# Block sums made in DRAM by accumulating transfers, and a fourth pair by seven products

## The chip, the cores and the metric

The kernel runs on one core of one Trainium2 chip. A core has five engines that run side by side, each with its own in-order queue: TensorE (PE, matrix products into PSUM), VectorE (DVE), ScalarE (ACT), GpSimd (POOL) and SyncE (SP, which here only issues transfers). Sixteen DMA engines move data between DRAM and SBUF for all queues. The metric is the time of one execution on the device in microseconds (us), the median of the runs; less is better.

## The reference

One layer of an encoder block on 256 tokens of width 2048, float32. What bears on the change is the output projection; everything else is shortened.

```
hn = rmsnorm(h, mix_norm_pre)
z, xbc, dt_raw, u = split(hn @ w_in)
y_ssd  = ssd_mixer(z, xbc, dt_raw, ...)        # 256 x 1024
y_pool = pool_mixer(u, pool_w, pool_scale)     # 256 x 1024
mix = concat([y_ssd, y_pool]) @ w_out          # 256 x 2048 times 2048 x 2048
h = h + rmsnorm(mix, mix_norm_post)
h = h + rmsnorm(conv_glu(rmsnorm(h, ...), w_up, w_down), ...)
h = h + rmsnorm(sigmoid(rmsnorm(h, ...) @ w_gate) * (p @ w_ple), ...)
```

## The kernel before

**Products.** Every float32 weight page is split into a high and a low part (ScalarE copies the high part, VectorE subtracts to get the low part, lines 157 and 158), and a product of x and w is three matmuls: high by high, high by low, low by high. A weight page is 128 partitions by 2048 columns, 1 MB; it holds a pair of contraction blocks of 128 rows by 1024 output columns, cut into four blocks of 512 columns. Three raw buffers (`raw`), five buffers for split weights (tag `w`), thirteen 1 MB pages (tag `pg`) hold the data.

**Plain pairs and pairs by seven products.** A plain pair takes 2 blocks x 2 token halves x 2 column blocks x 3 matmuls = 24 matmuls of 128x512. A pair may instead be done by a scheme of the Strassen and Winograd kind with seven block products, 21 matmuls (`seven_products`, line 277). That needs sums of the four weight blocks (`add_blocks`: block 1 += block 0; block 0 += block 3; block 3 += block 1; block 2 += block 3, in this order) and four sums of the operand (`pair_sums`). Its splits are named after the pair: a (block 1, 512 columns) and b (blocks 2 and 3) come from the raw page, d and c (the sums) from a second page `t` where the sums were made earlier, or else from the raw page after `add_blocks` has run over it. One combining step (`combine`) follows the last fast pair of a half.

**The output projection** (`wo`) runs as two halves of 1024 output columns, eight pairs each. The lists of pairs are numbered by their first block k; the second half goes through the blocks 8, 10, 12, 0, 2, 14, 4, 6. By seven products go the pairs 0 and 2 of the first half and 12, 0, 2 of the second. For four of these five the sums are made early, in the stages of `xbc` (the three slabs 2, 0, 1) and `z`: `early_fetch` loads the weight page into a page `wob`, `early_add` adds on VectorE (line 275) and stores the page to DRAM (`wos`, line 265, a GpSimd transfer); the projection loads it again as `wo00t`, `wo02t`, `wo10t`, `wo12t`. Pair 12 makes its sums in the projection itself, on its raw page `wo112r`.

**What sets the order.** `aside()` runs the next list of `work` after each pair of a stage, so a job's place in `work` says in which part of a stage it is written. The Tile scheduler then orders each engine's queue by priority. SyncE's loads also keep the order of `issue_after(last["dma"])`: a load that waits for a buffer holds those behind it. GpSimd's queue carries the stores, and between them the small instructions of the norms, among them `yn0m`, `yn0r`, `yn1m`, `yn1r` (lines 410 to 417 and 817), the norm of y: y is scaled by them on VectorE, turned by TensorE (`y_turn`, tile `yt`, line 827) and becomes the operand of the pairs 0 to 6.

Of the kernel before, what the change touches and what calls it, by code (L numbers as in the profile page):

```python
# [11 lines left out]
F32 = mybir.dt.float32  # L12
F32R = mybir.dt.float32r
AF = mybir.ActivationFunctionType
ALU = mybir.AluOpType
ORDERED = (mybir.EngineType.Activation, mybir.EngineType.DVE, mybir.EngineType.SP)

P = 128
# [20 lines left out]
V_MIX, V_SCW, V_SCB, V_SN, V_PS, V_FN = 0, 16, 76, 88, 96, 104  # L39
# [14 lines left out]
def build(nc, a, out):  # L54
    x = a["x"][0]

    w_dtu, w_xbc, w_z, w_out, w_up = a["w_dtu"], a["w_xbc"], a["w_z"], a["w_out_"], a["w_up"]
# [3 lines left out]
    with tile.TileContext(nc) as tc, \  # L61
# [9 lines left out]
        def ins(r):  # L71
            return getattr(r, "ins", r)

        def page(name, dtype=F32):
            return gp.tile([P, 2048], dtype, tag="pg", bufs=13, name=name)

        def mid(name, dtype=F32):
            return gp.tile([P, 1024], dtype, tag="mid", bufs=3, name=name)
# [4 lines left out]
        def main(name):  # L83
            return [pm.tile([P, 512], F32, tag="main", name=f"{name}_{i}") for i in range(2)]
# [30 lines left out]
        last, sums_ = {}, {}  # L115

        def load(dst, src, ahead=False):

            with tc.issue_after(last["dma"]) if last and not ahead else nullcontext():
                return ins(nc.sync.dma_start(dst, src))  # L120
# [79 lines left out]
        work = []  # L200
# [31 lines left out]
        def block_sums(name, w, c0, k, held):  # L232


            pg = []

            def fetch():
                r = page(f"{name}b{c0}_{k}")
                pg.append(r)
                load(r, w[c0 // 1024, k // 2])  # L240

            def add():
                add_blocks(pg[0])
                if held:
                    sums_[name, c0, k] = pg[0], True

            def store():
                if not held:
                    t = dp.tile([P, 2048], F32, tag=f"{name}s{c0}_{k}", bufs=1, name=f"{name}s{c0}_{k}")
                    nc.gpsimd.dma_start(t, pg[0])  # L250
                    sums_[name, c0, k] = t, False

            return fetch, add, store

        early_raw = {}

        def early_fetch(c, k):
            early_raw[c, k] = page(f"wob{c}_{k}")
            load(early_raw[c, k], w_out[c, k // 2])

        def early_add(c, k):
            r = early_raw.pop((c, k))
            add_blocks(r)
            t = dp.tile([P, 2048], F32, tag=f"wos{c}_{k}", bufs=1, name=f"wos{c}_{k}")
            nc.gpsimd.dma_start(t, r)
            sums_["wo", c * 1024, k] = t, False

        APART = ("dn",)

        def add_blocks(r, t=None):  # L270

            v = r.rearrange("p (b c) -> p b c", b=4)
            s = v if t is None else t.rearrange("p (b c) -> p b c", b=4)
            for i, a, b in ((1, v, 0), (0, v, 3), (3, s, 1), (2, s, 3)):
                nc.vector.tensor_add(s[:, i], v[:, i], a[:, b])  # L275
# [95 lines left out]
        def feature_major(name, w, get, acc):  # L371

            for u in range(4):
                r = raw(f"{name}r{u}", w[u])
                for j in range(2):
                    wh, wl = split(f"{name}{u}_{j}", r[:, j * 1024:(j + 1) * 1024], 1024)
                    for kk in range(2):
                        k = 4 * u + 2 * j + kk
                        xh, xl = get(k)
                        for f in range(4):  # L380
                            s = slice(kk * 512 + f * P, kk * 512 + (f + 1) * P)
                            for q, (ww, xx) in enumerate(((wh, xh), (wh, xl), (wl, xh))):
                                mm(acc[f // 2][:, f % 2 * L:(f % 2 + 1) * L], ww[:, s], xx,
                                   k == 0 and q == 0 and f % 2 == 0, k == NK - 1 and q == 2)
                aside()
# [19 lines left out]
        def rms(name, parts, scale, n=1):  # L405

            base = EPS
            for i, q in enumerate(parts):
                m = tiny(f"{name}m{i}", n)
                nc.gpsimd.tensor_scalar(m, q, scale, base, op0=ALU.mult, op1=ALU.add)  # L410
                base = m
            r = tiny(f"{name}r", n)
            nc.gpsimd.tensor_tensor(r, m, mhalf[:, :n], op=ALU.pow)
            return r
# [36 lines left out]
        def times_rows(name, acc, rb):  # L451
            o = mid(name)
            for i in range(2):
                nc.vector.tensor_tensor(o[:, i * 512:(i + 1) * 512].rearrange("p (f t) -> p f t", f=2),
                                        acc[i].rearrange("p (f t) -> p f t", f=2),
                                        rb.unsqueeze(1).to_broadcast([P, 2, L]), op=ALU.mult)
            return o

        def conv(name, acc, taps, wcol, wstep, bcol):

            cv = mid(name)
            half = taps // 2
            for f in range(4):
                o, i = cv[:, f * L:(f + 1) * L], acc[:, f * L:(f + 1) * L]
                nc.scalar.activation(o, i, AF.Identity, bias=vec(bcol + f), scale=vec(wcol + half * wstep + f))
                for j in range(taps):
                    d = j - half
                    if d == 0:
                        continue
                    lo, hi = max(0, -d), L - max(0, d)  # L470
                    nc.vector.scalar_tensor_tensor(o[:, lo:hi], i[:, lo + d:hi + d], vec(wcol + j * wstep + f),
                                                   o[:, lo:hi], op0=ALU.mult, op1=ALU.add)
            return cv
# [15 lines left out]
        for u in range(0, NK, 2):  # L489
            r = [wp.tile([P, 2048], F32, tag="raw", bufs=3, name=f"dtur{u}") if u else r0, page(f"dtur{u + 1}")]  # L490
            for j in range(2):
                k = u + j
# [17 lines left out]
            for j in range(2):  # L510
                k = u + j
# [129 lines left out]
        cat = Panel.__new__(Panel)  # L641
# [54 lines left out]
        def xbc(slab):  # L696
            acc = main(f"xbc{slab}")
            feature_major(f"xb{slab}", w_xbc[slab], hn, acc)
            sc = times_rows(f"xr{slab}", acc, rxb)
            cv = conv(f"cv{slab}", sc, 5, V_SCW + 4 * slab, 12, V_SCB + 4 * slab)  # L700
            th = mid(f"th{slab}")
            nc.scalar.activation(th, cv, AF.Tanh, scale=0.5)

            nc.vector.scalar_tensor_tensor(cv, th, 1.0, cv, op0=ALU.add, op1=ALU.mult)
            return cv
# [42 lines left out]
        def job(f, *args):  # L748
            return lambda: f(*args)
# [5 lines left out]
            [job(pool_mix, 2), job(pool_mix, 3), job(decays), job(seg_sums)],  # L755
            [],
        ])
        work[0].append(job(early_fetch, 0, 0))
        work[2].append(job(early_add, 0, 0))
        work[1].append(job(early_fetch, 0, 2))  # L760
        work[3].append(job(early_add, 0, 2))
        work[3].append(job(early_fetch, 1, 0))
        bc = xbc(2)
        work.extend([
            [job(seg, 0), job(seg, 1), job(pool_map, 0), job(pool_map, 1)],
# [1 line left out]
            [job(seg, 4), job(weigh, 0, 0), job(pool_map, 2)],  # L767
            [job(seg, 5), job(pool_map, 3)],
        ])
        work[0].append(job(early_add, 1, 0))  # L770
        xa = xbc(0)
        work.extend([
            [job(seg, 6)],
# [1 line left out]
            [job(xs_turn, xa, 0)],  # L775
            [],
        ])
        xb = xbc(1)
        y = page("y")

# [8 lines left out]
            [job(mix, 0, 1), job(mix, 1, 0)],  # L789
            [job(mix, 1, 1)],  # L790
        ])
        work[4].append(job(early_fetch, 1, 2))
        work[6].append(job(early_add, 1, 2))
        zacc = [main(f"z{t}") for t in range(2)]
        token_major("z", w_z, 0, list(range(NK)), hn, zacc)
        assert not work
# [5 lines left out]
        for t in range(2):  # L802
# [13 lines left out]
            r = rms(f"yn{t}", [ss], rz[t][:, 1:2], n=2)  # L816
# [16 lines left out]
        def gload(name, src):  # L833
            g = cp.tile([P, D], F32, tag="gain", name=name)
            load(g, src.partition_broadcast(P))
            return g
# [91 lines left out]
        for t in range(2):  # L928
            load(h[t], x[t * P:(t + 1) * P, :])
        hf = sublayer("wo", w_out, (list(range(8, 16)) + list(range(8)), [8,9,10,11,12,13,0,1,2,3,14,15,4,5,6,7]), cat, gload("gmix", a["mix_norm_post"][0]), h,  # L930
                      V_FN, Pairs, ((4,5),(2,3,4)), Sums("cs", cat))


        pl = [ple(0)]
# [39 lines left out]
        for i, w_ in enumerate(which[2:] + which[:2]):  # L974
            fetch, add, store = block_sums(*w_, i >= len(which) - 2)
            n = 45 * i // 10 + 4
# [110 lines left out]
        with in_order():  # L1087
            for _ in range(5):
                next_part()
            for n in range(NPIECES):  # L1090
                s, v, i = blocks[n // 4]
# [135 lines left out]
        for half in range(2):  # L1227
# [16 lines left out]
            for t in range(2):  # L1244
                for n, (o, c0) in enumerate(columns(acc[t])):
                    c1 = c0 + o.shape[-1]
                    c = slice(half * 1024 + c0, half * 1024 + c1)

                    th = mid(f"gth{half}{t}{n}")
                    v = th[:, :c1 - c0]  # L1250
# [103 lines left out]
```

## Time and profile before

| what | us |
|---|---|
| median of 3 runs (1105.19 to 1105.71) | 1105.4 |
| the profiled execution | 1104.97 |
| its span | 1103.2 |
| TensorE busy | 1096.7 |
| VectorE busy | 977.2 |
| ScalarE busy | 729.1 |
| GpSimd busy | 84.9 |

The span is what the profiler saw between the first and the last instruction; the time of the profiled execution is 1.8 us longer. The stages that the change touches lie between 50 and 284 us: xbc to about 141, z to 196, the first half of the projection to 241, the second half to 284. In a row of the profile, "out<-in" names the tiles that an instruction writes and reads, xN counts, and what stands in brackets is the idle time before it with what ended that time.

### The profile page before, as it was taken

How to read it: one execution, taken by the hardware profiler on the slowest of the kernel's cores; microseconds unless marked ns; L12 is line 12 of the kernel's file. 1: busy time of each engine (PE TensorE's matmuls, PEld its weight loads, DVE VectorE, ACT ScalarE, POOL GpSimd, SP SyncE). 2: the span in 40 equal slices, each digit the busy share in tenths (PEclk: the TensorE clock that was granted, in tenths of full speed). 3: DMA queues.
4: the chain of work that ended last, by engine and by line, in shares of the span. 5: the costliest groups of instructions: out<-in, count | busy, mean ns of one | idle time of the engine just before them, and what ended most of it. 6: DMA issues, size and time to landing. Idle time of an engine off the chain costs nothing.

```text
span 1103.2 us, 16052 instructions
## 1 busy us (share of the span) xinstructions
PE 1096.7 (99%) x5961; PEld 948.8 (86%) x5961; DVE 977.2 (89%) x1373; ACT 729.1 (66%) x1068; POOL 84.9 (8%) x145
## 2 busy tenths in 40 slices
PE   9999999999999999999999999999999999999998
PEld 9999988888888888888888888888888888888886
DVE  6589998898868998889889988898999999999997
ACT  6858763566776565655656646657688878786773
POOL 0200000100100000000000000000000000051001
PEclk9999999999999999999999999999999999999999
DMA  9895259556489999989999998999999989996872
GB/s 363 359 339 195 101 183 367 209 195 244 158 367 388 408 397 364 403 344 367 383 366 383 364 391 345 404 362 420 367 410 375 378 335 389 419 379 224 317 276 77
DMA packets 57247, 361.71 MB, mean 328 GB/s; under 512 B 6352, under 2 KB 7504, under 8 KB 21200
## 3 DMA queue, kind: packets, MB, share of 16 engines
q1 hardware_dynamic: 45648, 298.71, 69.0%
q0 software_dynamic: 11088, 61.35, 14.5%
q8 instruction: 47, 0.77, 0.3%
q10 hardware_dynamic: 432, 0.62, 0.2%
q14 instruction: 32, 0.26, 0.1%
HBM read 306.65 MB, written 54.00 MB: 327 GB/s over the span
## 4 chain that ended last, share of the span: by engine, by line
PE 97%; ACT 1%; DVE 1%; issue 0%; POOL 0%; POOLq 0%; DVEq 0%
PE ga L90 22%; PE va L90 22%; PE dna L90 11%; PE woa L90 7%; PE xbc L90 5%; PE gt L90 5%; PE dns L90 4%; PE dtu L90 4%; PE z L90 4%; PE dn0s L90 2%; PE dn1s L90 2%; PE ple L90 1%; PE gts L90 1%; PE wos L90 1%; PE yd L90 1%; PE pw L90 1%
## 5 line engine op out<-in xcount | busy, mean ns | idle before, releaser
L90 PE MATMUL ga<-wox,ug_0w 128*128 128x512 f32 x704 | 130.8, 337 | 0.0
L90 PE MATMUL ga<-wox,ug_1w 128*128 128x512 f32 x704 | 130.2, 337 | 0.0
L90 PE MATMUL va<-wox,uv_0w 128*128 128x512 f32 x704 | 129.2, 337 | 0.0
L90 PE MATMUL va<-wox,uv_1w 128*128 128x512 f32 x704 | 129.2, 337 | 0.0
L90 PEld LDWEIGHTS ga<-wox,ug_0w 128*128 128x128 f32 x704 | 107.7, 188 | 14.6 <-ACT pl L919 0.2
L90 PEld LDWEIGHTS ga<-wox,ug_1w 128*128 128x128 f32 x704 | 107.5, 188 | 14.5 <-DVE wox L195 0.2
L90 PEld LDWEIGHTS va<-wox,uv_1w 128*128 128x128 f32 x704 | 107.5, 188 | 14.5
L90 PEld LDWEIGHTS va<-wox,uv_0w 128*128 128x128 f32 x704 | 107.5, 188 | 14.5
L275 DVE TENSOR_TENSOR dnb<-dnb 128x512 f32<-128x512 f32 x128 | 88.3, 690 | 3.0
L250 POOL DMA_DIRECT2D dns<-dnb x30 | 16.1, 536 | 319.4 <-DVE dnb L275 279.1
L90 PE MATMUL xbc<-hnh,xb_0w 128*128 128x256 f32 x192 | 37.9, 284 | 0.3 <-ACT u L571 0.3
L90 PE MATMUL xbc<-hnh,xb_1w 128*128 128x256 f32 x192 | 37.1, 283 | 0.0
L846 ACT CAST he<-he 128x512 fp32r<-128x512 f32 x13 | 8.1, 621 | 42.6 <-DVE he L845 42.6
L988 ACT CAST hs<-hid 128x384 fp32r<-128x384 f32 (+1 forms) x44 | 23.4, 537 | 13.7 <-PE dna L90 13.5
L90 PEld LDWEIGHTS xbc<-hnh,xb_0w 128*128 128x128 f32 x192 | 30.8, 189 | 0.9 <-ACT u L571 0.4
L90 PEld LDWEIGHTS xbc<-hnh,xb_1w 128*128 128x128 f32 x192 | 30.7, 189 | 0.1
L1068 ACT ACTIVATE fc<-gr,vt 128x256 f32<-128x256 f32 x44 | 26.1, 593 | 6.9 <-DVE gr L1061 6.9
L90 PE MATMUL dna<-dn_0w,hs 128*128 128x512 f32 x108 | 28.6, 394 | 0.0
L90 PE MATMUL dna<-dn_1w,hs 128*128 128x512 f32 x108 | 28.3, 392 | 0.0
L1139 POOL DMA_DIRECT2D hd<-hsum x24 | 12.9, 539 | 193.1 <-PE dn0s L90 70.4
L989 DVE TENSOR_TENSOR hs<-hid,hs 128x384 fp32r<-128x384 f32 (+1 forms) x44 | 25.4, 581 | 2.6 <-ACT hs L988 2.6
L90 PE MATMUL xbc<-hnl,xb_1w 128*128 128x256 f32 x96 | 27.3, 284 | 0.0
(1781 smaller groups left out, 2871.4 us busy)
## 6 DMA issues: line engine op xcount, KB each, us to landing
dnb<-w_down SPq DMA_DIRECT2D x32, 1024.0 KB, 10.0
dns<-dnb POOLq DMA_DIRECT2D x30, 1024.0 KB, 6.5
hd<-hsum POOLq DMA_DIRECT2D x24, 512.0 KB, 8.2
zr<-w_z SPq DMA_DIRECT2D x8, 1024.0 KB, 5.0
dtur<-w_dtu SPq DMA_DIRECT2D x14, 528.0 KB, 8.5
hsum<-he POOLq DMA_DIRECT2D x13, 512.0 KB, 7.7
wo0r<-w_out_ SPq DMA_DIRECT2D x6, 1024.0 KB, 6.2
gtb<-w_gate SPq DMA_DIRECT2D x6, 1024.0 KB, 9.6
```

Of the source, the lines that this page charges most:

```text
L90: last["pe"] = ins(nc.tensor.matmul(o, lhsT, rhs, start=start, stop=stop, skip_group_check=True))
L250: nc.gpsimd.dma_start(t, pg[0])
L275: nc.vector.tensor_add(s[:, i], v[:, i], a[:, b])
L846: nc.scalar.copy(o[:, :512], s[:, :512])
L988: nc.scalar.copy(t[:, :c1], hid_part(k)[:, :c1])
L989: nc.vector.tensor_sub(t[:, 512:512 + c1], hid_part(k)[:, :c1], t[:, :c1].bitcast(F32))
L1068: nc.scalar.activation(c[:, f], v[:, f], AF.Identity, bias=vec(V_FCB + 4 * s + 2 * i + f), scale=vec(w + NF))
L1139: nc.gpsimd.dma_start(o.bitcast(F32), kept[k])
```

## The change

`early_fetch` and `early_add` go. In their place `sums_in_dram(c, k)` gives three jobs, placed in consecutive lists of `work`: a copy of the weight page from DRAM to DRAM (SyncE's queue), two accumulating transfers on GpSimd's queue that add block 3 to the copy's blocks 0 and 2 and block 0 to its blocks 1 and 3 (512 KB each), and two more that add block 1 of the copy to its block 2 and block 1 of the weights to its block 3 (256 KB each). VectorE and the pages `wob` are not used for it. It is done for six pairs: those four, pair 12 of the second half, and pair 10 of the second half, which is now done by seven products too.

```diff
-        def early_fetch(c, k):
-            early_raw[c, k] = page(f"wob{c}_{k}")
-            load(early_raw[c, k], w_out[c, k // 2])
-
-        def early_add(c, k):
-            r = early_raw.pop((c, k))
-            add_blocks(r)
+        def sums_in_dram(c, k):
             t = dp.tile([P, 2048], F32, tag=f"wos{c}_{k}", bufs=1, name=f"wos{c}_{k}")
-            nc.gpsimd.dma_start(t, r)
-            sums_["wo", c * 1024, k] = t, False
+            src = w_out[c, k // 2]
+            o, v = (u.rearrange("p (b c) -> p b c", b=4) for u in (t, src))
+
+            def add(dst, from_):
+                nc.gpsimd.dma_start(dst, from_, accum_op=ALU.add)
+
+            def copy():
+                load(t, src)
+
+            def pairs_():
+                add(o[:, 0::2], v[:, 3:4].to_broadcast([P, 2, 512]))
+                add(o[:, 1::2], v[:, 0:1].to_broadcast([P, 2, 512]))
+
+            def rest():
+                add(o[:, 2], o[:, 1])
+                add(o[:, 3], v[:, 1])
+                sums_["wo", c * 1024, k] = t, False
+
+            return copy, pairs_, rest
...
-        work[0].append(job(early_fetch, 0, 0))
-        work[2].append(job(early_add, 0, 0))
-        work[1].append(job(early_fetch, 0, 2))
-        work[3].append(job(early_add, 0, 2))
-        work[3].append(job(early_fetch, 1, 0))
+        for n, j in enumerate(sums_in_dram(0, 0)):
+            work[1 + n].append(j)
...
-        work[0].append(job(early_add, 1, 0))
+        for n, j in enumerate(sums_in_dram(0, 2)):
+            work[1 + n].append(j)
...
+        for n, j in enumerate(sums_in_dram(1, 0)):
+            work[1 + n].append(j)
...
-        work[4].append(job(early_fetch, 1, 2))
-        work[6].append(job(early_add, 1, 2))
+        for n, j in enumerate(sums_in_dram(1, 2)):
+            work[1 + n].append(j)
+        for n, j in enumerate(sums_in_dram(1, 10)):
+            work[5 + n].append(j)
+        for n, j in enumerate(sums_in_dram(1, 12)):
+            work[3 + n].append(j)
...
-                      V_FN, Pairs, ((4,5),(2,3,4)), Sums("cs", cat))
+                      V_FN, Pairs, ((4,5),(1,2,3,4)), Sums("cs", cat))
```

Two places in the queues. SyncE's loads for the second half of the projection, before (a name wo1NNr is the raw page of pair NN, wo1NNt its sums; wo1r are raw pages of plain pairs):

```order
L120 DMA wo1r_2468<-w_out_ 128x2048
L120 DMA wo1r_2500<-w_out_ 128x2048
L120 DMA wo112r<-w_out_ 128x2048
L120 DMA wo10r<-w_out_ 128x1536
L120 DMA wo12r<-w_out_ 128x1536
L120 DMA wo10t<-wos_0_1073 128x2048
L120 DMA wo12t<-wos_2_2005 128x2048
L120 DMA wo1r_2656<-w_out_ 128x2048
```

and in the changed kernel:

```order
L120 DMA wo1r_2472<-w_out_ 128x2048
L120 DMA wo110r<-w_out_ 128x1536
L120 DMA wo112r<-w_out_ 128x1536
L120 DMA wo10r<-w_out_ 128x1536
L120 DMA wo110t<-wos_10_1667 128x2048
L120 DMA wo112t<-wos_12_1668 128x2048
L120 DMA wo10t<-wos_0_1362 128x2048
L120 DMA wo12r<-w_out_ 128x1536
L120 DMA wo12t<-wos_2_1666 128x2048
```

The second pair of the half, 10, now has a page of sums, and its load stands behind three raw pages, the last of which takes the buffer of the half's first pair.

GpSimd's queue ahead of the norm of y, at the end of the z stage, before:

```order
L608 TENSOR_TENSOR dec<-dec,dt 128x16 x2
L265 DMA wos_2_926<-wob_2_763 128x2048
L265 DMA wos_0_1073<-wob_0_928 128x2048
L265 DMA wos_2_2005<-wob_2_1890 128x2048
L410 TENSOR_SCALAR yn0m_2069<-ss_2060,rz_2055 128x2
L413 TENSOR_TENSOR yn0r<-yn0m_2069,mhalf 128x2
```

and in the changed kernel:

```order
L262 DMA wos_2_1666<-w_out_ 256x1x512 x2
L262 DMA wos_2_1666<-wos_2_1666 128x512
L262 DMA wos_2_1666<-w_out_ 128x512
L262 DMA wos_12_1668<-w_out_ 256x1x512 x2
L262 DMA wos_12_1668<-wos_12_1668 128x512
L262 DMA wos_12_1668<-w_out_ 128x512
L262 DMA wos_10_1667<-w_out_ 256x1x512 x2
L262 DMA wos_10_1667<-wos_10_1667 128x512
L262 DMA wos_10_1667<-w_out_ 128x512
L420 TENSOR_SCALAR yn0m_2073<-ss_2064,rz_2059 128x2
L423 TENSOR_TENSOR yn0r<-yn0m_2073,mhalf 128x2
```

Twelve accumulating transfers of the three last blocks now stand ahead of `yn0m` in the z stage, each block's second two behind a wait for its first two, and its first two behind a wait for its copy; before, one store stood there.

More of the change, by code (lines that the diff above doesn't have):

```diff
@@ L253, in block_sums @@
             return fetch, add, store
-        early_raw = {}
-        def early_fetch(c, k):
-            early_raw[c, k] = page(f"wob{c}_{k}")
-            load(early_raw[c, k], w_out[c, k // 2])
-        def early_add(c, k):
-            r = early_raw.pop((c, k))
-            add_blocks(r)
-            t = dp.tile([P, 2048], F32, tag=f"wos{c}_{k}", bufs=1, name=f"wos{c}_{k}")
-            nc.gpsimd.dma_start(t, r)
-            sums_["wo", c * 1024, k] = t, False
+        def sums_in_dram(c, k):
+            t = dp.tile([P, 2048], F32, tag=f"wos{c}_{k}", bufs=1, name=f"wos{c}_{k}")
+            src = w_out[c, k // 2]
[12 more added lines that the diff above has]
+            return copy, pairs_, rest
         APART = ("dn",)
```

## The prediction

> **What bounds the kernel now.** I read the page first, then the chain of waits, then the table of windows, then the rows of single queues around the change.
>
> ```profile
> span 1103.2 us, 16052 instructions
> PE 1096.7 (99%) x5961; PEld 948.8 (86%) x5961; DVE 977.2 (89%) x1373; ACT 729.1 (66%) x1068; POOL 84.9 (8%) x145
> PE 97%; ACT 1%; DVE 1%; issue 0%; POOL 0%; POOLq 0%; DVEq 0%
> ```
>
> The chain that ended last is 97% TensorE. That is an average, so the stages that the change touches come from the windows (us; busy time and instructions of PE, PEld, DVE, ACT, POOL; granted clock; DMA share; GB/s):
>
> ```profile
> 50.00:64.00 14.00, 13.75 (x112) 13.55 (x111) 13.74 (x27) 9.39 (x13) 0.53 (x1) 1.00 0.68 261
> 64.00:79.00 15.00, 15.00 (x126) 14.53 (x125) 12.30 (x23) 6.49 (x10) 1.50 (x3) 1.00 0.96 358
> 79.00:90.00 11.00, 10.82 (x88) 10.46 (x87) 9.13 (x19) 10.96 (x17) 1.12 (x2) 1.00 0.73 282
> 90.00:120.00 30.00, 29.98 (x232) 28.89 (x231) 28.96 (x55) 23.39 (x46) 0.00 (x0) 1.00 0.39 135
> 120.00:141.00 21.00, 21.00 (x172) 20.55 (x171) 20.73 (x36) 13.47 (x25) 0.00 (x0) 1.00 0.40 142
> 141.00:163.00 22.00, 22.00 (x99) 17.97 (x98) 21.62 (x44) 15.79 (x30) 0.00 (x0) 1.00 0.45 168
> 163.00:175.00 12.00, 12.00 (x56) 9.72 (x55) 11.96 (x12) 4.98 (x6) 0.00 (x0) 1.00 0.94 371
> 175.00:186.00 11.00, 11.00 (x63) 8.98 (x61) 8.26 (x11) 3.14 (x3) 0.53 (x1) 1.00 0.87 333
> 186.00:197.00 11.00, 11.00 (x63) 9.14 (x62) 7.36 (x12) 4.97 (x9) 1.93 (x5) 1.00 0.58 223
> 241.00:284.00 43.00, 43.00 (x187) 34.76 (x186) 36.96 (x46) 25.32 (x33) 1.81 (x6) 1.00 0.68 255
> ```
>
> TensorE is full in every one of them: from 50 to 197 us it lacks 0.25 + 0.18 + 0.02 = 0.45 us in all, and in the second half of the output projection (241 to 284) nothing. VectorE is nearly as full in places (21.62 of 22). So time comes back only where TensorE has fewer products, and it is lost only where something makes TensorE wait that does not now.
>
> **Term 1, three products fewer.** The chain in the second half, start and length in us:
>
> ```profile
> 240.78 11.55 PE woa L90 x50
> 252.34 0.69 PE wos L90 x3
> 257.22 0.70 PE wos L90 x3
> ```
>
> A plain product takes 11.55 / 50 = 0.231 us, so a plain pair, 24 products, 5.54. The second and third row are the first products of pair 12 and of pair 0: a pair by seven products, 21 of them, lies 4.88 apart. Pair 10 goes from the one to the other: **-0.66 us**.
>
> **Term 2, VectorE's adds.** The change takes away both of these groups:
>
> ```profile
> L275 DVE TENSOR_TENSOR wob<-wob 128x512 f32<-128x512 f32 x16 | 11.0, 686 | 0.2
> L275 DVE TENSOR_TENSOR wo112r<-wo112r 128x512 f32<-128x512 f32 x4 | 2.7, 686 | 0.1
> ```
>
> The sixteen lie in the stages above, where TensorE is full anyway; all that they could give back is the 0.45 us, and I take 0. In the second half 2.7 us go, and pair 10 brings two more splits (0.7 + 3 x 1.22 against 2 x 1.22 us, by the split rows below) and its own operand sums (0.69 + 4 x 0.29 + 0.68, as pair 12 has them): about 1.9 + 2.5 - 2.7 = 1.7 us more for a VectorE with 6 us spare. Hidden, unless it comes late at the first fast pair, which is term 3.
>
> **Term 3, the first fast pair is one pair earlier and its sums are a load.** SyncE's issues, TensorE's gate and what the splits cost (start, length in us):
>
> ```profile
> 239.69 0.33 SPq L120 DMA_DIRECT2D wo10r<-w_out_  x1
> 243.50 0.42 SPq L120 DMA_DIRECT2D wo10t<-wos  x1
> wo10t<-wos SPq DMA_DIRECT2D x1, 1024.0 KB, 6.7
> wo02t<-wos SPq DMA_DIRECT2D x1, 1024.0 KB, 10.2
> 250.19 1.05 ACT L157 CAST wo112dw<-wo112r 128x1024 fp32r<-128x1024 f32 x1 [2.69 <-DVE wo112r L275]
> 251.27 1.22 DVE L158 TENSOR_TENSOR wo112dw<-wo112r,wo112dw 128x1024 fp32r<-128x1024 f32 x1 [1.17 <-ACT wo112dw L157]
> 253.54 0.68 DVE L158 TENSOR_TENSOR wo10aw<-wo10r,wo10aw 128x512 fp32r<-128x512 f32 x1
> ```
>
> In the new order wo110t is issued right behind wo10r, which waits for a raw buffer until 239.69. Issued at 240.1, and landing after 6.7 us as wo10t did behind a raw page, it is there at 246.8. TensorE reaches pair 10 at 252.34 - 5.54 = 246.8, and its first nine products (a11, a12, s4) need wo110r alone: the sums' first high part is wanted at 246.8 + 9 x 0.232 = 248.9, its low part four products later, at 249.8. ScalarE has the high part at 246.8 + 1.05 = 247.9, VectorE the low part at 249.1. That is 0.7 to 1.0 us of room. Behind it VectorE goes on with 112's splits, and by the same durations ends its third (112d) at about 253.1, where TensorE wants it at 253.5. So nothing to 1 us is lost; between these ends I take **+0.2 us**. The far end is a landing like wo02t's 10.2 us: 3.5 us later, 2.5 to 2.8 of them seen.
>
> **Term 4, six sums made in DRAM.** Each block is copied (1 MB, SyncE's queue), then gets two accumulating transfers of 512 KB and two of 256 KB from GpSimd. No row shows either kind. What all transfers between 50 and 200 us cost:
>
> ```profile
> DMA packets 4722, 34.14 MB, mean 228 GB/s; under 512 B 531, under 2 KB 531, under 8 KB 659
> q1 hardware_dynamic: 4134, 29.78, 53.0%
> q0 software_dynamic: 576, 4.19, 7.1%
> wos<-wob POOLq DMA_DIRECT2D x4, 1024.0 KB, 4.7
> ```
>
> 60.1% of 150 us for 34.14 MB is 2.64 us per MB. By the windows' shares 58 of the 147 us from 50 to 197 are free, and the pages that are no longer fetched and stored (some 8 MB) free about 20 more. Lower bound, every new byte priced like the old: 6.3 MB copied and 9.4 MB added, 15.7 x 2.64 = 41 us. Upper bound, a copy twice (it reads and writes DRAM) and an add three times: 40.9 x 2.64 = 108 us. The rows priced are also transfers that read one side and write the other, so I take the copy once, and the add twice, for its second read: 66 us against 78 free. It fits, without much room. A weight page has some: the third one of z is issued at 134.86 and lands 6.0 us later,
>
> ```profile
> 134.86 0.33 SPq L120 DMA_DIRECT2D zr<-w_z  x1
> zr<-w_z SPq DMA_DIRECT2D x1, 1024.0 KB, 6.0
> 140.67 22.09 PE z L90 x96
> 162.76 0.87 PE xt L693 x8
> ```
>
> and its products begin at 140.67 + 2 x 5.52 = 151.7, after a split of 2.3 us: 8.5 us of slack. So **0**; with the cover gone it is rival A.
>
> GpSimd's queue matters more than the bytes. Its instruction for the norm of y stands behind the last accumulating issue:
>
> ```profile
> 128.77 0.33 SPq L120 DMA_DIRECT2D zr<-w_z  x1
> 138.23 0.33 SPq L120 DMA_DIRECT2D zr<-w_z  x1
> 150.74 0.33 SPq L120 DMA_DIRECT2D zr<-w_z  x1
> 178.37 0.53 POOL L265 DMA_DIRECT2D wos<-wob  x1 [91.11 <-DVE wob L275]
> 194.98 0.58 POOL L410 TENSOR_SCALAR yn0m<-ss,rz 128x2 f32<-128x2 f32 x1 [16.09 <-ACT zt L815]
> 202.32 1.46 POOL L410 TENSOR_SCALAR yn1m<-ss,rz 128x2 f32<-128x2 f32 x1 [4.85 <-ACT zt L815]
> 207.41 0.44 PE yt L827 x4
> ```
>
> The three copies of the z stage are issued behind these three z pages and land at about 139, 148 and 161 (two 5 us transfers in a row each). Per block GpSimd then waits for the two 512 KB adds: 1.05 MB x 2 x 2.64 = 5.5 us alone, say 11 in company. The last issue is then at about 161 + 11 = 172, and 23 us remain to 194.98. The issues themselves are 0.53 us. The Trainium skill's page SBUF — State Buffer (section "A bandwidth-pool intuition that's wrong (but worth ruling out)") says that a VectorE instruction which holds the port it shares with GpSimd keeps GpSimd from writing descriptors, so that a GpSimd transfer of 620 ns took 3100 ns beside it. The trace of before does not show it: the issue above took 0.53 us with VectorE busy for 8.26 of 11 us.
>
> **Sum.** -0.66 + 0.2 = -0.46 us. The profiled execution took 1104.97 us for its span of 1103.2, and lies 0.43 below the median of the runs, 1105.4; the difference carries over to the median: **1105.0 us**.
>
> **Rivals.**
> A, slower: **GpSimd is held by the accumulating transfers** until after the norm of y is due. It decides from about 20 us per pair of 512 KB adds on (139 + 3 x 20 = 199, between 194.98 and 202.32), 3.6 times my 5.5. At 25 us GpSimd is free at 214, yn1r comes 13 us later than its 205.0, and the transposes at 207.41, which have 1.5 us of room, hold TensorE for about 11: 1105.4 - 0.7 + 11 = 1116. For it: an unseen kind of transfer, and the upper bound of 108 us does not fit into 78. Against it: its threshold is far from any row. 0.15.
> A', **each issue is long** because VectorE is busy: 2.5 us more for each of twelve issues of the last three blocks would put the last one at 172 + 30 = 202; yn0m begins there, yn1r ends at about 207 and the transposes come 1 to 2 us late: 1106.5. The 0.53 us speaks against it. 0.03. By the Trainium skill's rule on that shared port, cited above, a delay of 2.5 us an issue (an estimate from its 620 and 3100 ns) would make this the outcome.
> B, **the sums of pair 10 are late**: wo110t lands like wo02t, 2.6 us lost, 1.9 net of term 1: 1107.3. For it: wo110t now waits behind wo10r's buffer, and VectorE is full. Against it: wo10t in the same position took 6.7. 0.10.
> C, **VectorE's relief is worth more than I see**, over 2.2 us: 1103. TensorE's 0.45 us of idle time speaks against it. 0.04.
> The forecast keeps 0.68.
>
> **How the numbers follow.** About 0.2%, 2.2 us, is what a measurement of this kernel can tell from no change. The forecast's own range is 1104.0 (term 1 with all of the 0.45 and the spread of the runs) to 1105.8 (term 3 at 1 us). To hold eight in ten it is widened to A' and B: 1104.0 to 1107.4, which leaves out A and C, 0.19. Faster by over 0.2%: C, 0.04. Slower: A and a third of B, 0.18. Within: 0.78.
>
> **What would show it.** Term 1: 21 products of pair 10 in 4.9 us and TensorE's count down by three; 2: no change of TensorE's idle time before 197 us; 3: the landing of wo110t by 247.5 and no wait of TensorE at its first sum product; 4: zr pages that land within 10 us, and GpSimd's last accumulating issue before 190 us. It is wrong if yn0m begins after 200 us, or if TensorE waits for more than 1 us anywhere between 50 and 284.

## The result, and the profile after

The changed kernel takes 1125.36 us (median of 5 runs, 1123.58 to 1125.95) against 1105.4: a ratio of 1.0178, 95% interval 1.0165 to 1.0191. It is slower by 20 us. The prediction had 1105.0 us, no change.

The page of the changed kernel: engines, the chain that ended last by engine, GpSimd's queue (packets, MB, share of 16 engines' span), and the first two accumulating transfers of each block (KB each, median us to landing):

```profile
PE 1100.2 (98%) x5958; PEld 949.4 (85%) x5958; DVE 969.5 (86%) x1361; ACT 728.5 (65%) x1071; POOL 105.4 (9%) x165
q0 software_dynamic: 15504, 66.59, 19.1%
PE 85%; DMA 7%; issue 3%; DVE 2%; ACT 2%; POOL 1%; SPq 0%; POOLq 0%; DVEq 0%; ACTq 0%
wos<-w_out_ POOLq DMA_DIRECT2D x12, 512.0 KB, 17.0
```

and that queue's row on the page before:

```profile
q0 software_dynamic: 11088, 61.35, 14.5%
```

TensorE was 97% of the chain and is now 85%; 7% are DMA, 5% of it `wos<-w_out_` and 1% an xbc page, `xb0r`. The three matmuls that term 1 removes are gone from the count. GpSimd's queue takes 19.1% of 1123.3 = 214.6 us of all 16 engines against 160.0. Before, the four stores took 7.1% of 150 = 10.7 us of this. So the accumulating transfers took 214.6 - 149.3 = 65 us for their 9.44 MB: **6.9 us per MB**. The prediction had 5.3.

Where TensorE lost it, from the windows of the changed kernel (columns as in the prediction):

```profile
64.00:79.00 15.00, 13.10 (x108) 12.56 (x108) 8.25 (x9) 7.30 (x10) 4.17 (x6) 1.00 1.01 337
141.00:163.00 22.00, 22.00 (x106) 18.35 (x105) 20.15 (x41) 14.79 (x29) 3.80 (x4) 1.00 1.02 297
163.00:175.00 12.00, 12.00 (x58) 9.87 (x58) 8.69 (x10) 4.11 (x6) 0.00 (x0) 1.00 1.04 271
186.00:197.00 11.00, 10.13 (x58) 8.39 (x58) 9.52 (x14) 3.23 (x6) 3.83 (x4) 1.00 0.94 228
196.00:241.00 45.00, 32.42 (x144) 26.03 (x143) 24.48 (x42) 16.99 (x28) 6.16 (x11) 0.85 0.67 208
```

All through the z stage the DMA engines are full (0.94 to 1.04, a share as the profile counts it; before 0.45 between 141 and 163), and in the worst part at fewer GB/s per share: 271 at 1.04, where before 371 went at 0.94. In the first half of the projection TensorE stands still for 12.6 of 45 us, and the granted clock is 0.85. GpSimd's queue and TensorE's waits say why (start, length; idle time before in brackets):

```profile
138.61 2.11 POOL L262 DMA_DIRECT2D wos<-w_out_  x2 [14.07 <-DMA wos<-w_out_]
159.09 0.82 POOL L262 DMA_DIRECT2D wos<-wos  x1 [18.38 <-issue]
159.62 3.27 POOL L262 DMA_DIRECT2D wos<-w_out_  x3
186.57 0.82 POOL L262 DMA_DIRECT2D wos<-wos  x1 [23.68 <-issue]
187.19 3.21 POOL L262 DMA_DIRECT2D wos<-w_out_  x3
212.09 0.82 POOL L262 DMA_DIRECT2D wos<-wos  x1 [21.69 <-issue]
...
213.85 0.26 POOL L420 TENSOR_SCALAR yn0m<-ss,rz 128x2 f32<-128x2 f32 x1
```

```profile
PE yt L841 <- DVE y L834: 12.6, 2, 7.6
PE mx L90 <- DVE mixl L665: 1.7, 1, 1.7
...
PE woa L90 <- ACT wo110dw L157: 0.3, 1, 0.3
PE wos L90 <- ACT wo110cw L157: 0.2, 1, 0.2
```

From a block's first two adds to its next two pass 20.5, 26 and 25 us. The second add of the two lands 0.5 us ahead of each of these issues (158.59, 186.07 and 211.59), so that GpSimd waits for the adds, though the rows say "issue". `yn0m`, written behind the last of them, begins at 213.85 instead of 194.98, y is late, and its transposes hold TensorE for 12.6 us, in two pauses. They have a second price, in TensorE's rows:

```profile
216.08 0.45 PE L841 MATMUL yt<-ident,y 128*128 128x128 f32 x1 [4.99 <-DVE y L834]
224.13 0.90 PE L841 MATMUL yt<-ident,y 128*128 128x128 f32 x3 [7.60 <-DVE y L834]
227.39 1.91 PE L90 MATMUL woa<-wo_0w,cath 128*128 128x512 f32 x4
229.85 1.08 PE L90 MATMUL woa<-wo_1w,cath 128*128 128x512 f32 x4
```

Four products take 1.91 us behind the second pause and 1.08 from 229.85 on (granted clock 0.52 from 224 to 230): 5.7 us at half speed, about 2.8 lost. (The Trainium skill, TensorE: Matmul & The Clock Gate, section "Part 1: The HAM clock gate", says that the array falls to half its clock when idle and needs a busy window of about 3.4 us to come back; the trace agrees, with the longer 5.7 us.)

The account, by starts of the same work before and after: the projection begins at 199.80 instead of 196.12 (+3.7); the turn of y adds 12.6 and the slow products about 3, so that the last transpose lies 19.3 later; the down projection begins 19.4 later (801.0 against 781.6); the end of the span is 20.1 later. So nearly all of the loss lies ahead of the last transpose.

### The profile page after: what moved, and what is told of

Read it like the earlier page. It is cut to its first block, busy times and chain, and to the rows that moved or that the text cites. A ratio compares the mean times of both kernels' runs of the same rounds, so it can differ in the third digit from the quotient of the medians.

```text
span 1123.3 us, 16065 instructions
## 1 busy us (share of the span) xinstructions
PE 1100.2 (98%) x5958; PEld 949.4 (85%) x5958; DVE 969.5 (86%) x1361; ACT 728.5 (65%) x1071; POOL 105.4 (9%) x165
## 3 DMA queue, kind: packets, MB, share of 16 engines
q0 software_dynamic: 15504, 66.59, 19.1%
## 4 chain that ended last, share of the span: by engine, by line
PE 85%; DMA 7%; issue 3%; DVE 2%; ACT 2%; POOL 1%; SPq 0%; POOLq 0%; DVEq 0%; ACTq 0%
PE ga L90 22%; PE va L90 22%; PE dna L90 11%; PE gt L90 5%; DMA wos<-w_out_ 5%; PE dns L90 4%; PE woa L90 4%; PE dtu L90 4%; PE dn0s L90 2%; PE xbc L90 2%; PE dn1s L90 2%; DMA xb0r<-w_xbc 1%; PE ple L90 1%; PE gts L90 1%; PE wos L90 1%
## 5 line engine op out<-in xcount | busy, mean ns | idle before, releaser
L90 PE MATMUL xbc<-hnl,xb_0w 128*128 128x256 f32 x96 | 27.3, 284 | 0.0
```

The source lines that it names most:

```text
L90: last["pe"] = ins(nc.tensor.matmul(o, lhsT, rhs, start=start, stop=stop, skip_group_check=True))
```

## The experiments

Each time is a median, beside runs of the kernel before on the same chip.

### The fourth pair alone

```diff
 # before.py
-                      V_FN, Pairs, ((4,5),(2,3,4)), Sums("cs", cat))
+                      V_FN, Pairs, ((4,5),(1,2,3,4)), Sums("cs", cat))
```

> The kernel before with only the fourth pair of the second half taken by seven products; its block sums are made by VectorE in place when its weights come, as the kernel before makes those of pair 12, and no sum is made in DRAM. If the seven products are worth what the prediction's first term says, TensorE saves 0.66 us and pays at most 0.2 us at the place of the first sums: 1104.7 to 1105.0 us, and the whole loss of the changed kernel comes from the sums in DRAM. If the fourth pair itself costs (four adds of some 0.69 us each on VectorE between 241 and 284 us, where it is busy 37 of 43 us), TensorE waits in the second half: 1106 us or more.

1110.9 us against 1105.03 (ratio 1.0051, 1.0032 to 1.0070): 5.9 us **slower**. The rival held. The chain of waits in the second half is VectorE's row of work, almost without a gap (`wo110r` and `wo112r` at L275 are the adds in place):

```profile
248.34 1.05 ACT wo110dw L157
...
254.11 0.61 DVE wo112r L275
...
257.00 1.05 ACT wo112dw L157
258.10 0.79 PE woa L90
```

TensorE waits 2.7 us there for pair 12's sums and 1.0 for pair 10's, and runs slowly behind the longer wait (granted clock 0.57 from 258 to 262 us, about 1.7 us lost): 5.4 in all, by which the next stage also begins later (295.45 instead of 290.06). So the fourth pair needs its sums made elsewhere; the sums in DRAM were not an addition to it but its condition.

### GpSimd's order

The last two adds of pair 12 and all four of pair 10 are put behind the norm of y:

```diff
 # after.py
-        for n, j in enumerate(sums_in_dram(1, 10)):
-            work[5 + n].append(j)
-        for n, j in enumerate(sums_in_dram(1, 12)):
-            work[3 + n].append(j)
+        s10, s12 = sums_in_dram(1, 10), sums_in_dram(1, 12)
+        for n, j in ((3, s12[0]), (4, s12[1]), (5, s10[0])):
+            work[n].append(j)
...
+        with tc.issue_after(normed):       # the last small instruction of the norm of y
+            for j in (s12[2], s10[1], s10[2]):
+                j()
```

> The changed kernel with nothing altered but GpSimd's order: the last two adds of pair 12 and all four accumulating transfers of pair 10 are put behind the norm of y, so that the norm no longer waits for them. Theory (GpSimd held): the waits of TensorE for y before the first turn (12.6 us) go, and with them the 2.9 us by which its products ran slowly after the pause; what stays is the 3.7 us lost up to the end of the z stage: 1109.5 us, 1108 to 1111. Rival (the transfers fill the DMA engines, and the wait for y is only where it shows): the weights or the sums come late instead, 1117 us or more.

1121.0 us against 1105.03 (1.0139, 1.0114 to 1.0165): only some 4 of the 20 us come back. The wait for y is gone, as the theory said; the rest is the rival's. From the chain and from TensorE's waits:

```profile
169.26 15.91 DMA wo0r<-w_out_
...
217.14 16.38 DMA wo00t<-wos
```

```profile
PE woa L90 <- ACT wo00dw L157: 4.6, 1, 4.6
PE yd L90 <- DVE y L756: 2.8, 1, 2.8
```

The first page of the projection takes 15.9 us to land beside pair 12's adds, and the load of `wo00t`, 8.1 us before, takes 16.4 beside pair 12's last and pair 10's first adds, which now run from 214 on. Behind both waits the granted clock drops (0.84 from 183 to 204 us, 0.57 from 232 to 240). GpSimd's order was the place where the time showed; the cause is the DMA engines' time.

### Four blocks instead of six

The two loops over `sums_in_dram(1, 10)` and `(1, 12)` are left out; VectorE makes those sums in place.

> The changed kernel with four of the six sums made in DRAM: the pairs 10 and 12 of the second half get theirs from VectorE in place, so that the z stage holds one block of accumulating transfers instead of three. Theory (GpSimd held by three blocks in a row): its last accumulating issue lies near 160 us, the norm of y starts near 198, TensorE does not wait for y; only the 3.7 us up to the end of the z stage stay: 1108.5 to 1110.5 us. Rival (any accumulating transfers beside the weight loads of the z stage do it): 1115 us or more.

1114.16 us (1.0079, 1.0054 to 1.0103). TensorE no longer waits for y, as expected, so three blocks of adds, in the xbc stage, and one in the z stage do not hold the norm. The time missed the 1108.5 to 1110.5 expected because the 5.9 us of the fourth pair with VectorE's sums are in it; above the run of that pair alone stand 3.3 us, and most of them are one wait in the xbc stage:

```profile
PE mx L90 <- DVE mixl L665: 2.6, 1, 2.6
```

### Plain transfers in place of accumulating ones

```diff
 # after.py
-                nc.gpsimd.dma_start(dst, from_, accum_op=ALU.add)
+                nc.gpsimd.dma_start(dst, from_)
```

> The changed kernel with its accumulating transfers replaced by plain ones of the same size, source, target, queue and waits; the additions of the block sums are left out. If adding in the transfer is what makes it long (about 8 us of all 16 engines per MB in the traced windows against 2.64 for the rest), a pair of 512 KB lands in about 11 us as the prediction had it, GpSimd is free before 190 us and the time is 1106 to 1109 us. If it is the path from DRAM to DRAM on GpSimd's queue, or the company of the weight loads, the pairs still take 20 to 26 us and the time stays at 1120 us or more.

1108.97 us (1.0034, 1.0019 to 1.0049): the accumulating form is worth some 16 of the 20 us. The times spread from 1106.35 to 1113.53, so a landmark in the traces is the better measure, the first products of the last fast pair's last sums, before, in the changed kernel and here (shortest, median and longest in ns, first and last start in us):

```profile
L90 PE MATMUL wos<-wo12cw,csp x3: 393/395/397, 265.5 to 265.9; 128*128 128x512 f32 x3
L90 PE MATMUL wos<-wo12cw,csp x3: 392/395/397, 284.9 to 285.4; 128*128 128x512 f32 x3
L90 PE MATMUL wos<-wo12cw,csp x3: 392/395/398, 267.2 to 267.7; 128*128 128x512 f32 x3
```

Of 19.4 us lost up to there 1.7 stay. (The traced execution is the one of 1113.53 us. Most of what it loses beyond that lies in a stage that the change does not touch: from the first `ga` product to the first of the down projection pass 496.1 us, before 491.6, and TensorE waits for nothing in it. Why is open.) In the stretch from 109 to 131 us the same 1.57 MB on GpSimd's queue, in the changed kernel:

```profile
q0 software_dynamic: 832, 1.57, 51.9%
```

and with plain transfers:

```profile
q0 software_dynamic: 448, 1.57, 25.7%
```

That is 11.4 against 5.7 us of 22, 7.3 against 3.6 us per MB: the accumulating form doubles it. Its packets are half as large: of the 832, 768 have 2,048 bytes and take 0.24 us each, of the 448 plain ones 384 have 4,096 bytes and take 0.23 (64 more of 4 bytes stand in either row); the loads and stores that the prediction took its price from go in packets of 8,192 bytes, 0.33 to 0.34 us each. Whether the smaller packets or a second read make a byte dearer is not separated: no run has plain packets of 2,048 bytes on this queue. GpSimd is free for the norm long before it is due (last issue, then `yn0m`):

```profile
183.84 0.55 POOL L262 DMA_DIRECT2D wos<-w_out_  x1
197.14 0.58 POOL L420 TENSOR_SCALAR yn0m<-ss,rz 128x2 f32<-128x2 f32 x1 [12.75 <-ACT zt L829]
```

### One block, in three places

The kernel before, with one of its sums made in DRAM instead of by VectorE and nothing else changed: pair 0 of the second half in the empty stretch around 110 us; pair 0 of the first half in the full stretch from 38 to 80 us; pair 12 in the z stage.

```diff
 # before.py with sums_in_dram; the first of the three
-        work[3].append(job(early_fetch, 1, 0))
-        work[0].append(job(early_add, 1, 0))
+        for n, j in enumerate(sums_in_dram(1, 0)):     # behind xbc(0), as in the changed kernel
+            work[1 + n].append(j)
```

> The kernel before with one of its four stored sums, pair 0 of the second half, made in DRAM by accumulating transfers, issued where the changed kernel issues them, around 110 to 130 us, where the DMA share before is 0.14 to 0.6. Theory (an accumulating MB takes some 7 us of all 16 engines, and this costs only where a load that TensorE needs runs beside it): nothing is late, 1104.7 to 1105.5 us. Rival (accumulating transfers slow the kernel wherever they stand, through GpSimd or the memory): 1106.5 us or more.

> The kernel before with one stored sum, pair 0 of the first half, made in DRAM, issued where the changed kernel does it, between 38 and 80 us, where the DMA share before is 0.7 to 1.0 and the loads of the second part of the xbc weights are due. The same volume as in the run with one block in the gap. Theory (collision with the weight loads): TensorE waits some 2 to 3 us between 70 and 80 us, 1107 to 1109 us. Rival (the place does not matter): the same time as the block in the gap.

> The kernel before with the sum of pair 12 of the second half made in DRAM, issued at 153 to 190 us beside the last z weights and the first weights of the output projection, where the changed kernel has three blocks in a row. Theory (the loss there is a queue: three blocks of some 11 us of all DMA engines each, where 20 us are free): one block fits into the free time, its last transfer is issued before 190 us, the norm of y starts by 198 us: 1104.7 to 1106 us. Rival (one block beside these loads is enough to hold the norm or the weights): 1109 us or more.

| place | us | ratio to 1105.59 |
|---|---|---|
| empty stretch | 1105.99 | 1.0003 (0.9995 to 1.0012) |
| full stretch | 1113.79 | 1.0070 (1.0057 to 1.0083) |
| z stage | 1107.67 | 1.0020 (1.0005 to 1.0035) |

The same 1 MB copied and 1.57 MB added cost nothing in one place and 8 us in another (in the empty stretch 0.4 us more, no difference that can be measured). In the empty stretch, first pair of adds, next issue:

```profile
104.97 2.21 POOL L275 DMA_DIRECT2D wos<-w_out_  x2 [25.00 <-DMA wos<-w_out_]
119.05 0.82 POOL L275 DMA_DIRECT2D wos<-wos  x1 [11.87 <-DMA wos<-w_out_]
```

Beside one or two weight loads, a pair takes 14 us (in the changed kernel 12.6 in the same stretch, from 110.24 to 122.87), and meanwhile the DMA share is 0.99: the stretch is empty only before and behind it. In the full stretch, from the chain, the waits and the windows:

```profile
54.41 14.12 DMA xb2r<-w_xbc
```

```profile
PE mx L90 <- DVE mixl L678: 3.0, 1, 3.0
```

```profile
70.00:76.00 6.00, 2.99 (x18) 2.78 (x17) 5.96 (x7) 4.54 (x6) 0.90 (x2) 0.76 0.87 146
```

The last page of the first xbc slab lands after 14.1 us instead of 5.8, TensorE stops, and its clock drops with it. This run came out worse than the 2 to 3 us expected, and worse than the 3.7 us that the changed kernel loses up to the projection. A difference is that the fetch of pair 2's page is still there: in this chain it lands 10.7 us after its issue, and VectorE's adds on it follow. In the z stage one block leaves y on time, as its theory said, but the time lies above the 1106 expected and below the rival's 1109. The projection begins where it did (196.23 us, before 196.12); 1.4 us are lost up to the next stage (291.49 instead of 290.06), where TensorE waits 0.9 us for the load of pair 12's sums. The rest is not placed.

### The sums of pair 10 by VectorE, stored

```diff
 # before.py, fourth pair as above
-        work.extend([[], [job(y_turn, 0)], [job(y_turn, 2), job(y_turn, 4)], [job(y_turn, 6)]])
+        work.extend([[], [job(y_turn, 0), job(early_fetch, 1, 10)], [job(y_turn, 2), job(y_turn, 4)],
+                     [job(y_turn, 6), job(early_add, 1, 10)]])
```

> The kernel before with the fourth pair by seven products, as in the run of the fourth pair alone, but the block sum of pair 10 is fetched, added by VectorE and stored during the first half of the output projection, as the kernel before does for its four stored sums; nothing is accumulated by a transfer. Theory (the fourth pair alone cost 5.9 us because eight adds of block sums stood in VectorE's row of work from 237 to 258 us): with pair 10's sum ready before, the row is shorter by four adds, TensorE waits at most 0.5 us there, and the 0.66 us of the seven products show: 1104.3 to 1105.3 us. Rival (the earlier place of the first fast pair costs, whoever makes the sum; or the adds only move the crowding to the turn of y, 205 to 220 us): 1107 us or more.

1115.46 us (1.0088, 1.0075 to 1.0102): the theory failed, and the time is in the rival's range, but the trace shows a third reason, the order of the loads. The fetch stands ahead of `wo00t`, and `wo110t` is issued behind `wo12r`, 7 us later than in the run with two sums below (240.53). From the chain:

```profile
247.86 6.49 DMA wo110t<-wos
```

TensorE waits 5.3 us for pair 10's sums, and the granted clock is 0.94 from 241 to 300 us.

### The fourth pair with one or two sums in DRAM, in the emptier stretches

```diff
 # before.py with sums_in_dram, fourth pair as above
+        for n, j in enumerate(sums_in_dram(1, 10)):    # behind xbc(0)
+            work[1 + n].append(j)
...
+        for n, j in enumerate(sums_in_dram(1, 12)):    # z stage; left out in the run with one sum
+            work[1 + n].append(j)
```

> The kernel before with the fourth pair by seven products and only the two sums that this needs made in DRAM: pair 10 at 105 to 125 us and pair 12 at 131 to 165 us, where the DMA engines are least busy; the four stored sums stay with VectorE. Theory (the fourth pair is worth 0.66 us if its sums and those of pair 12 are off VectorE's row of 237 to 258 us, and an accumulated block costs nothing where the engines are free): TensorE waits at most 1 us in all between 50 and 290 us, 1104.4 to 1106 us. Rival (two more loads of sums behind the first raw load of the second half, or the room of the pages, keep TensorE waiting): 1107.5 us or more.

> As the run with two sums in the gap, but pair 12's sum is made by VectorE in place, as in the kernel before, and only pair 10's in DRAM. Theory (VectorE's row): four of the eight adds that stood in it when the fourth pair came alone (5.9 us lost) are gone; the row ends 2.7 us sooner, so that about half or more of that loss goes: 1105 to 1108 us, not below the run with two. Rival (the loss of the fourth pair alone was not VectorE's row): 1110 us or more, as there.

With two sums: 1104.93 us against 1105.12 (ratio 1.0003, 0.9993 to 1.0014), no difference that can be measured, and no wait of TensorE from 50 to 290 us but an old one of 0.2. Its last fast pair's last sums begin at 265.3 us (265.5 before), though z began 0.4 later: the 0.6 us of term 1 are there by this one trace of each kernel, and too small to show in the time. GpSimd's rows, with the norm due at 195 (the first two adds of the block were issued at 136.87):

```profile
154.74 0.83 POOL L275 DMA_DIRECT2D wos<-wos  x1 [15.76 <-DMA wos<-w_out_]
...
195.39 0.58 POOL L433 TENSOR_SCALAR yn0m<-ss,rz 128x2 f32<-128x2 f32 x1 [14.49 <-ACT zt L842]
```

With one sum: 1110.47 us (1.0050, 1.0038 to 1.0062). Here the theory missed: half of VectorE's adds were gone and nearly nothing came back. The chain:

```profile
240.44 7.45 DMA wo110t<-wos
247.91 1.06 ACT wo110dw L157
...
253.09 0.61 DVE wo112r L298
...
258.03 0.50 PE wos L90
```

VectorE's row is shorter, but it starts only when `wo110t` lands at 247.9, and pair 12's four adds still stand in it behind pair 10's splits. By this chain the loss is less the number of adds than that pair 12's stand between two fast pairs 5 us apart. TensorE's waits in this trace, 2.9 us, do not make up the whole 5.4: the next stage begins 3.2 later (293.21 instead of 290.06), and the rest stays open.

## Why the prediction was wrong

Its own signs of being wrong all came: `yn0m` after 200 us, the last accumulating issue after 190, TensorE waiting more than 1 us between 50 and 284. Two of the z pages took 12.2 and 16.8 us to land, against the 10 that it named, but TensorE did not wait for them: slack was there, as it had reckoned for one of them. **The step that failed is term 4**, "So 0", and within it the sentence "5.5 us alone, say 11 in company". The runs show 12.6 to 14 us for a pair in the emptiest stretch and 20 to 26 in the z stage of the changed kernel, so that GpSimd was held and y came late: 15.4 us lost there, with 3.7 ahead of the projection, where the step had put nothing. Three things went wrong in it.

- The price. An added MB was taken at 5.3 us of all 16 engines ("the add twice, for its second read"); it took 6.9. The bounds had it inside. The price came from packets of 8,192 bytes, and the accumulating ones have 2,048. The copies were priced rightly: SyncE's queue moved 3.7 MB more than before in 9.4 us more.
- The place. 66 us were set against 78 free over the whole stretch from 50 to 197. But three of the six blocks stand in the z stage, where by the windows of before 12.1 + 0.7 + 1.4 + 4.6 = 19 us were free, and 5.5 more with pair 2's page gone. Three blocks at the prediction's own price need 3 x 11.1 = 33 us, at the measured one 41. Done for the stage, the sum would have shown a lack of 9 us even with the price too low. The lack of 16.5 by the measured price, an estimate, lies near the 15 us by which the norm of y was late beyond the 3.7 us already lost. The runs with one block in three places show how much the place matters: the same volume costs from nothing to 8 us.
- The queue. The slack of one z page, 8.5 us, was taken for all loads. Time was lost at pages that the prediction had not looked at: xb0r (12.7 us to land, before 5.8) in the xbc stage, xb2r in the run with one block there, and the first page of the projection (14.2 us, before 10.2).

**Rival A** (0.15, 1116 us) named the mechanism, its threshold ("from about 20 us per pair") and, at 25 us, GpSimd free "at 214"; it was free at 213.75, and TensorE waited 12.6 us where A said about 11. A was short by 9 us: it left out the 3.7 us lost before the projection and the half clock after the pauses, some 3. Its argument against itself, "its threshold is far from any row", was no evidence: no row showed an accumulating transfer, the threshold of 20 us is 3.6 times the 5.5 but only 1.8 times the 11 that the prediction itself used, and "the upper bound of 108 us does not fit into 78" should have weighed more. The run with GpSimd's order changed shows that A is not the cause either but the outlet: with the norm ahead, the 12.6 us of waits and the slow products behind them are gone, but waits of 4.6 and 2.8 us for loads, each with slow products behind it, come in their place.

**Rival A'** fell: the issues took 1.22 us (from the weights) and 0.83 (from the copy) in the median, more than the 0.53, but plain transfers at the same places took 0.68 and 0.53 beside the same work of VectorE, so that the accumulating form is what lengthens it. The 2.5 us more by the Trainium skill's rule on the shared port were not seen in any of these issues' medians.

**Term 1** was right: 0.6 us, seen only where nothing else is late. (The prediction's sum, 1105.4 - 0.46, gives 1104.9 rather than 1105.0, which changes nothing.) **Term 3** was right in size: `wo110t` landed 7.8 us after its issue (6.7 taken), and TensorE waited 0.5 us at pair 10's sums, within 0 to 1, though it had named "no wait" as its sign. **Term 2** was right for this change, but its 0 hid what the adds cost otherwise: left to VectorE, pair 10's and pair 12's sums make the fourth pair 5.9 us slower. **B** and **C** did not happen.

## What to carry to other kernels

Free DMA time is a budget of each stage, not of a stretch of stages: set the new transfers of a stage against the free share of that stage, and look for every load due in it, before anything else. A stretch that is empty before the change is full while the new transfers run in it. An operation that no row shows should not be priced from the cheap end because it moves the same bytes; when its upper bound does not fit, that case is the forecast's rival with the weight. And moving a waiting instruction to another place in its queue only moves the loss if the engines behind it are full.

## What the runs showed of the hardware

An accumulating transfer from DRAM to DRAM took 6.9 us of all 16 DMA engines per MB over the program (7.3 in one stretch), a plain one on the same queue and with the same shapes 3.6 in that stretch. It went in packets of 2,048 bytes, the plain one in packets of 4,096, at 0.24 and 0.23 us each. Its issue took 1.22 or 0.83 us in the median, a plain one's 0.68 or 0.53. A 1 MB load that takes 5.8 us otherwise took 14.1 beside two accumulating transfers of 512 KB. Two pauses of TensorE, of 5.0 and 7.6 us, cost about 3 us more afterwards, at half its clock; a wait of 2.7 us, with the fourth pair alone, was already followed by a granted clock of 0.57 from 258 to 262 us.
